# A two-layer diffusion backbone on one core: order of work in layer 1's in-projection and at the program's end

## The chip, the cores and the metric

The kernel runs on one core of a Trainium2 chip. A core has a matrix unit, TensorE (PE in the profile, its weight loads PEld), three engines for elementwise work, VectorE (DVE), ScalarE (ACT) and GpSimd (POOL), and SyncE (SP), which issues most transfers here. Each engine runs its own list of instructions in order and waits on semaphores for the others. The metric is the device time of one execution in microseconds; the kernel before took 2872.38 us, the median of three runs (2871.62 to 2872.77).

## The reference, cut to what matters

The reference sends 1024 latent tokens and 256 context tokens, each 1024 wide, through two layers and a final RMSNorm of the latent tokens. The part that the change touches is layer 1's grouped-query attention up to the first scores, and the end of the program.

```python
hl, hc = modulate(xl, ...), modulate(xc, ...)   # rms_norm(x) * (1 + scale) + shift
pl = hl @ w_in                                  # 8 query heads, 2 key heads, 2 value heads of 128
ql = gqa_q(pl[..., :GQA_Q_W], g_q, cos, sin, True)
kl, vl = gqa_kv(pl[..., GQA_Q_W:], g_k, cos, sin, True)
kc, vc = gqa_kv(hc @ w_in[:, GQA_Q_W:], g_k, cos, sin, False)
ol = attention(ql, concat([kc, kl]), concat([vc, vl])) @ w_out
...
xl = xl + ml[:, 5] * conv_ffn(...)              # a = h @ w_up; (silu(conv(g)) * u) @ w_down
return rms_norm(xl, g_final)
```

Queries and keys are normalised per head over 128 values and then rotated (`apply_rope`); scores of a block are `q k / sqrt(128)`, and their softmax starts with a maximum over the 1280 keys.

## The kernel before, in words

All tokens lie with the model's width on the partitions, in eight tiles of 128 (index k). The tokens form three chunks: two latent ones of 512 columns (c = 0 and 1) and the context of 256 (c = 2). Every product of float32 numbers is made of three matmuls (L72): a value is split into a rounded high part and the rest, and high by high, high by low and low by high are added. So each operand costs a cast for its high part and a subtraction for its low part, besides the matmuls.

The stretches at issue are ordered by hand: inside a region opened with `manual_schedule` each engine executes its work in the order in which the program's calls are written (in the first of the two regions SyncE's transfers are placed by the scheduler, in the second by hand too). So moving a call moves its instructions on every engine that it uses.

*Layer 1's in-projection* is the region that opens at L2276. `Norm` (L1474) makes the RMSNorm and the modulation of one chunk: n0 for chunk 0, n2 for the context, n1 for chunk 1. Its `add` squares a tile on ScalarE (L1489 for the first, L1492 for the others) and adds it to the sum on the engine it is given (L1493); `split` casts the sum (L1505) and makes its low half (L1506); `total` adds over the partitions with a matmul by ones (L203, L204); `root` makes 1/sqrt on ScalarE in three steps, a scaled copy, a logarithm and an exponential (L167, L169, L170), and `rest` a Newton step of three operations on VectorE (L173 to L175). `modulate1` (L225), called in three parts a, b and c_, makes a modulated tile: the scaled value on VectorE (L236), its high part on ScalarE (L243) and its low part on VectorE (L249); for odd tiles of chunk 1 the scaling is on GpSimd (L238, L239) and the low part at L251.

Weights arrive as raw float32 (`wload`, L92); `split(eng)` casts a block's high part on ScalarE (L115) and makes its low part on the engine named (L111). `product(mt, c, ks)` is one block of 128 columns of queries (0 to 7) or keys (8, 9) times a chunk, over the k given, three matmuls each. `Key` and `Query` work on a product: its squares (L2425 for queries) and their split (L2426, L2427; L195, L196 for keys), `stat` with the matmul that sums them (L2436 for queries; L203, L204 for keys), `rope` with three operations on VectorE (L2355, L2358) and a sum on GpSimd (L2362), and `rest`, the Newton step. `value(t, k)` is the value product of token tile t, whose bank is called v, for the last two tiles T; `keep_value` casts it out of the bank (L2465) and makes its low half (L2466). Then attention begins: scores on TensorE (L1197 to L1199), maxima on VectorE (L1220), exponentials on ScalarE (L1237).

Small tiles come from `tmp` by tag: y has two buffers, z one, and some tags have one more from another pool here. A new tile of a tag waits until the last reader of the buffer's former content is done.

*The end* is the region that opens at L2905. It finishes the second layer's ConvFFN and the final norm in three pieces of columns, p (512), q and t (256 each). `prod(d)` is the last part of the down product of tile d (6 matmuls for p, 12 for q or t), `upd` adds it to the stream (L2096, VectorE), `sq` squares it (L2926), `add` sums the squares (L2929), `hi` and `lo` split the sum (L2933, L2936), `total`, `root` and `rest` are as above, `out(d, eng)` scales the tile (L2957 or L2959) and issues its store (L2960), and `pre` is a scaling on ScalarE that `out` on GpSimd needs (L2949).

ScalarE keeps one set of function tables at a time; a function that isn't in it makes an ACT_TABLE_LOAD. `tables(name, pinned)` (L283) asks for a set ahead of its use:

```python
i = S.preload_act_table_set(name)
if pinned:
    tc.keep_in_program_order(i)
```

The set `natural_log_exp_and_others` holds the functions of `root`.

## Time and profile before

| | |
|---|---|
| median of three runs | 2872.38 us (2871.62 to 2872.77) |
| the profiled execution's own time | 2870.99 us |
| its span in the profile | 2869.2 us |
| TensorE busy | 97% of the span |
| VectorE busy | 79% |
| ScalarE busy | 43% |
| GpSimd busy | 24% |
| mean granted clock of TensorE | 0.988 |

The in-projection's stretch of interest runs from 1594.4 to 1767.5 us in the profile, where attention's first exponential starts; the end's region begins on ScalarE at 2814.8 and the span ends at 2869.2. In a view of the timeline a row gives the start, the length, the engine, the line, the operation, the tiles and their shapes, how many instructions of that kind follow each other (xN), and in brackets how long the engine had stood idle and what ended that. In a table of windows each row gives a stretch, its length, and then for TensorE, its weight loads, VectorE, ScalarE and GpSimd the busy time and the number of instructions, then the granted clock (1.00 is the full one) and the share of the transfer engines.

### The profile page before, as it was taken

The numbers are of one execution on the slowest core, as the hardware profiler recorded it, in microseconds if no ns is written. First come the engines' busy times: TensorE is split into PE (matmuls) and PEld (weight loads), VectorE is DVE, ScalarE is ACT, GpSimd is POOL, SyncE is SP. The second block draws the span as 40 slices with busy tenths as digits, with TensorE's granted clock in tenths as the row PEclk, the third lists the DMA queues.
The fourth block names the chain that finished last, engine by engine and source line by source line (L and its number), as shares of the span: only waits on it lengthen the run. The fifth ranks groups of instructions, "written<-read, shape, count | busy, mean of one in ns | idle before, by whom it ended". The sixth has DMA issues, their size and how long they took to land.

```text
span 2869.2 us, 40136 instructions
## 1 busy us (share of the span) xinstructions
PE 2775.6 (97%) x14654; PEld 2318.1 (81%) x14654; DVE 2272.8 (79%) x3886; ACT 1241.0 (43%) x2518; POOL 700.2 (24%) x828
## 2 busy tenths in 40 slices
PE   7988999999999999999999998999999999999997
PEld 3856888887888888888888877999877788888886
DVE  5688888868888888778777787888758777779766
ACT  5525888824433333331002444888734333333104
POOL 2241444763000001011013443444330000001112
PEclk9999999999999999999999999999999999999998
DMA  6144001183143334363221010000041222226211
GB/s 230 71 142 140 15 24 59 57 290 124 41 138 132 126 124 136 132 239 96 69 72 51 29 37 23 1 2 1 27 141 54 81 88 81 75 101 232 92 59 59
DMA packets 97230, 264.89 MB, mean 92 GB/s; under 512 B 11908, under 2 KB 21060, under 8 KB 96904
## 3 DMA queue, kind: packets, MB, share of 16 engines
q1 hardware_dynamic: 97032, 262.33, 27.2%
q8 instruction: 115, 1.88, 0.3%
q14 instruction: 83, 0.68, 0.1%
HBM read 212.53 MB, written 49.75 MB: 91 GB/s over the span
## 4 chain that ended last, share of the span: by engine, by line
PE 64%; DVE 7%; ACT 2%; issue 1%; POOL 1%; DMA 0%; DVEq 0%; SPq 0%; ACTq 0%; POOLq 0%
PE d L72 18%; PE y L72 11%; PE z L72 7%; PE x L72 7%; PE p L72 6%; PE pv L1277 3%; PE b L72 3%; PE T L1264 2%; PE qk L72 1%; PE S L1197 1%; PE S L1199 1%; PE S L1198 1%; PE v L72 1%; DVE x L2014 0%; DVE mx L1220 0%
## 5 line engine op out<-in xcount | busy, mean ns | idle before, releaser
L2096 DVE SCALAR_TENSOR_TENSOR x<-d,mod,x 128x512 f32<-128x512 f32 (+1 forms) x352 | 254.5, 735 | 94.7 <-PE d L72 92.6
L1267 DVE TENSOR_TENSOR tl<-T,th 128x512 fp32r<-128x512 f32 x328 | 225.5, 687 | 46.8 <-ACT th L1266 42.1
L1277 PE MATMUL pv<-th,v 128*128 128x256 f32 x976 | 254.1, 309 | 1.4 <-ACT vo L1406 1.0
L1220 DVE TENSOR_REDUCE mx<-S 128x1 f32<-128x512 f32 (+1 forms) x400 | 233.9, 585 | 10.9 <-PE S L1199 3.7
L1246 POOL TENSOR_SCALAR p<-p,sm 128x1280 f32<-128x1280 f32 x128 | 171.2, 1338 | 288.1 <-DVE sm L1245 190.3
L72 PE MATMUL d<-act,wh 128*128 128x512 f32 (+1 forms) x832 | 231.8, 365 | 0.0
L1266 ACT CAST th<-T 128x512 fp32r<-128x512 f32 x328 | 192.2, 586 | 84.2 <-PE T L1264 76.5
L2079 ACT CAST act<-act 128x512 fp32r<-128x512 f32 (+1 forms) x110 | 61.5, 577 | 382.8 <-PE d L72 222.0
L72 PE MATMUL b<-h,wh 128*128 128x512 f32 (+1 forms) x752 | 206.5, 362 | 6.0 <-DVE h L489 4.1
L1678 POOL TENSOR_SCALAR a1h<-raw 128x1024 fp32r<-128x1024 f32 x38 | 43.2, 1138 | 675.4 <-DMA raw<-in_wup 457.7
L1698 ACT CAST s2h<-x 128x512 fp32r<-128x512 f32 x40 | 24.9, 622 | 392.5 <-PE x L72 254.9
L1264 PE MATMUL T<-ident,p 128*128 128x128 f32 x1280 | 193.0, 272 | 1.6 <-POOL p L1246 1.6
L72 PE MATMUL x<-h,a1h 128*128 128x512 f32 x608 | 191.2, 396 | 0.0
L1264 PEld LDWEIGHTS T<-ident,p 128*128 128x128 f32 x1280 | 156.5, 140 | 34.9 <-POOL p L1246 3.3
L1277 PE MATMUL pv<-tl,v 128*128 128x256 f32 x656 | 177.4, 282 | 0.0
L1277 PEld LDWEIGHTS pv<-th,v 128*128 128x128 f32 x976 | 173.4, 189 | 2.4 <-ACT vo L1406 1.5
L72 PEld LDWEIGHTS d<-act,wh 128*128 128x128 f32 x832 | 149.6, 189 | 27.2
L72 PEld LDWEIGHTS b<-h,wh 128*128 128x128 f32 x752 | 133.0, 189 | 35.8 <-DVE h L489 5.4
L72 PE MATMUL d<-act,wl 128*128 128x512 f32 (+1 forms) x416 | 151.8, 365 | 0.0
L1237 ACT ACTIVATE p<-S,mx,rq 128x512 f32<-128x512 f32 (+1 forms) x192 | 136.2, 712 | 12.7 <-DVE mx L1228 11.2
L72 PE MATMUL b<-h,wl 128*128 128x512 f32 (+1 forms) x376 | 135.8, 361 | 2.4 <-DVE wl L111 2.4
L72 PEld LDWEIGHTS x<-h,a1h 128*128 128x128 f32 x608 | 114.8, 189 | 26.6
(519 smaller groups left out, 7959.1 us busy)
## 6 DMA issues: line engine op xcount, KB each, us to landing
raw<-in_wup SPq DMA_DIRECT2D x86, 512.0 KB, 3.3
wm<-in_wmod SPq DMA_DIRECT2D x72, 512.0 KB, 3.6
act<-d_act SPq DMA_DIRECT2D x88, 256.0 KB, 3.5
raw<-in_wdn SPq DMA_DIRECT2D x44, 512.0 KB, 4.3
raw<-in_wout SPq DMA_DIRECT2D x32, 512.0 KB, 3.5
d_act<-su SPq DMA_DIRECT2D x22, 640.0 KB, 3.8
d_act<-su SPq DMA_DIRECT2D x22, 512.0 KB, 2.6
raw<-in_win SPq DMA_DIRECT2D x20, 512.0 KB, 3.6
```

The lines of the kernel that those rows point to most:

```text
L72: PE.matmul(out, w, x, start=first and i == 0, stop=last and i == n - 1, skip_group_check=more)
L1197: PE.matmul(o, qh, kh[:, ks], start=True, stop=False)
L1220: V.reduce_max(mx[:, j : j + 1], s, axis=AX.X)
L1237: S.activation(o, s, AF.Exp, scale=self.scale, bias=self.mx[:, 3:4], accum_out=self.sm[:, j : j + 1])
L1246: P.tensor_scalar(out=self.p, in0=self.p, scalar1=sm[:, 3:4], scalar2=1.0, op0=ALU.mult, op1=ALU.mult)
L1264: PE.transpose(tb[:, (2 * j + i) * 128 : (2 * j + i) * 128 + 128], rows[i].p[:, c : c + 128], ident)
L1266: S.copy(hi, tb)
L1267: V.tensor_sub(lo, tb, f32(hi))
L1277: PE.matmul(out[0], st, mv, start=(u + j == 0 and x == 0), stop=(u + j == n - 1 and x == len(ops) - 1))
L1678: P.tensor_scalar(out=hi[:, c], in0=self.raw[f, s][:, c], scalar1=1.0, scalar2=0.0, op0=ALU.mult, op1=ALU.add)
L2079: S.copy(hi, f32(lo))
L2096: V.scalar_tensor_tensor(out=x, in0=b, scalar=mod[self.l, c // 2][:, 40 + d : 41 + d], in1=x, op0=ALU.mult, op1=ALU.add)
```

## The change

Seven things are rearranged; every product and every sum stays.

1. The eight `n1.add` calls, of which the first only squares and the others square and add, have their seven sums on VectorE instead of GpSimd. Three calls stand ahead of n2's root and one behind it (three sums, all ahead of n2's Newton step on VectorE), four behind n2's last modulation; before, they were spread between n2's modulations.
2. Key 8's second half of its product with chunk 1, `product(8, 1, range(4, 8))`, stands ahead of `k8_0.stat`, which sums the squares of key 8 and chunk 0.
3. The rope's temporary is of tag z instead of y for queries from head 2 on.
4. Three weight splits stand earlier; `b4_0` stands ahead of `q1_0.stat`, and the statistics of q4_0 and q5_0 behind the product that followed them.
5. `keep_value(4)` and `keep_value(5)` stand together, ahead of the last query's statistics, rope and Newton steps.
6. The end's preload of the tables is pinned to its place in the region.
7. In the end, two more products of t stand ahead of `q.total`; t's sums of squares are all on VectorE; p's and q's outputs are placed later, four of q's behind t's low half, and q's tile 5 is scaled on VectorE.

```diff
--- before.py
+++ after.py
@@ -2348,10 +2348,10 @@
             qtiles[h, c] = hp.tile([128, 512], F32, name="q", tag="h", bufs=HB)
         return qtiles[h, c]
 
-    def rope1(b, c, gcol, dst, n):
+    def rope1(b, c, gcol, dst, n, tag="y"):
 
         c0 = CH[c][0]
-        t = tmp("y", n)
+        t = tmp(tag, n)
         V.scalar_tensor_tensor(out=t, in0=b, scalar=cols[:, gcol : gcol + 1], in1=rc[:, c0 : c0 + n], op0=ALU.mult, op1=ALU.mult)
         for d0 in (0, 64):
             s0 = 64 - d0
@@ -2438,7 +2438,7 @@
                 self.r, self.newton = roots(*i)
 
         def rope(self):
-            rope1(self.b, self.c, G1Q, q_of(self.h, self.c), 512)
+            rope1(self.b, self.c, G1Q, q_of(self.h, self.c), 512, "y" if self.h < 2 else "z")
 
         def rest(self):
             if self.h % 4 == 3:
@@ -2514,39 +2514,35 @@
     value(1, 5)
     value(0, 7)
     n2.total()
-    n1.add(P)
+    n1.add(V)
+    n1.add(V)
+    n1.add(V)
     n2.root()
+    n1.add(V)
     n2.rest()
     n2.a(0, False, "hi")
     n2.b(0)
     value(1, 7)
     value(2, 7)
-    n1.add(P)
     n2.a(1, False, "hi")
     n2.a(2, False, "lo")
-    n1.add(P)
     n2.a(3, False, "lo")
     n2.b(1)
     n2.c_(0)
     n2.b(3)
     n2.b(2)
     n2.c_(1)
-    n1.add(P)
     n2.c_(2)
-    n1.add(P)
     n2.a(4, False, "hi")
     n2.b(4)
     n2.c_(3)
-    n1.add(P)
     b8_0 = product(8, 0, range(0, 8))
     n2.a(5, False, "hi")
     n2.b(5)
     n2.c_(4)
-    n1.add(P)
     n2.a(6, False, "lo")
     n2.b(6)
     n2.c_(5)
-    n1.add(P)
     n2.a(7, False, "lo")
     n2.b(7)
     n2.c_(6)
@@ -2557,6 +2553,10 @@
     value(9, 2)
     value(8, 1)
     n2.c_(7)
+    n1.add(V)
+    n1.add(V)
+    n1.add(V)
+    n1.add(V)
     value(8, 4)
     value(9, 1)
     value(9, 3)
@@ -2615,9 +2615,9 @@
     k8_0 = Key(0, 0, b8_0)
     product(0, 0, range(4, 8), b0_0)
     b8_1 = product(8, 1, range(0, 4))
+    product(8, 1, range(4, 8), b8_1)
     k8_0.stat()
     k8_0.rope()
-    product(8, 1, range(4, 8), b8_1)
     b9_1 = product(9, 1, range(0, 4))
     k8_2 = Key(0, 2, b8_2)
     k8_2.stat()
@@ -2669,12 +2669,12 @@
     product(3, 1, range(4, 8), b3_1)
     q0_1.rope()
     q1_0 = Query(1, 0, b1_0)
+    split(P)
+    b4_0 = product(4, 0, range(0, 4))
     q1_0.stat()
-    split(P)
     q1_0.rope()
     k9_1.rest()
     k9_1.end()
-    b4_0 = product(4, 0, range(0, 4))
     q1_1 = Query(1, 1, b1_1)
     q1_1.stat()
     q1_1.rope()
@@ -2695,17 +2695,17 @@
     q3_0.stat()
     q3_0.rope()
     product(5, 0, range(4, 8), b5_0)
+    split(P)
     q3_0.rest()
     q3_1.stat()
     q3_1.rope()
     q4_0 = Query(4, 0, b4_0)
     q3_1.rest()
-    split(P)
     b5_1 = product(5, 1, range(0, 2))
     product(5, 1, range(2, 6), b5_1)
-    q4_0.stat()
     q4_0.rope()
     product(5, 1, range(6, 8), b5_1)
+    q4_0.stat()
     b6_0 = product(6, 0, range(0, 4))
     q4_1 = Query(4, 1, b4_1)
     split(P)
@@ -2713,9 +2713,9 @@
     q4_1.stat()
     q4_1.rope()
     q5_0 = Query(5, 0, b5_0)
-    q5_0.stat()
     q5_0.rope()
     b6_1 = product(6, 1, range(0, 2))
+    q5_0.stat()
     q6_0 = Query(6, 0, b6_0)
     product(6, 1, range(2, 6), b6_1)
     product(6, 1, range(6, 8), b6_1)
@@ -2735,8 +2735,8 @@
     q6_1.rope()
     product(7, 1, range(2, 6), b7_1)
     q7_0 = Query(7, 0, b7_0)
+    split(P)
     q7_0.stat()
-    split(P)
     q7_0.rope()
     product(7, 1, range(6, 8), b7_1)
     value(4, 0)
@@ -2759,14 +2759,14 @@
     value(4, 6)
     value(4, 7)
     q7_1 = Query(7, 1, b7_1)
-    q7_0.rest()
-    q7_1.stat()
-    q7_1.rope()
     value(5, 5)
     value(5, 7)
     keep_value(4)
+    keep_value(5)
+    q7_1.stat()
+    q7_1.rope()
+    q7_0.rest()
     q7_1.rest()
-    keep_value(5)
     close_ps()
     close_tp()
     close_n()
@@ -2905,7 +2905,7 @@
 
     regions.append(tc.manual_schedule(engines=ENGINES | {mybir.EngineType.SP}))
     regions[-1].__enter__()
-    tables("natural_log_exp_and_others", False)
+    tables("natural_log_exp_and_others")
 
     class Piece:
 
@@ -3031,59 +3031,59 @@
     q.add(7, V)
     q.hi()
     p.out(3, P)
+    t.prod(0)
     q.lo()
-    t.prod(0)
+    t.prod(1)
     p.out(5, P)
     t.upd(0)
     t.sq(0)
-    t.prod(1)
     t.upd(1)
+    t.sq(1)
+    t.prod(2)
+    t.prod(3)
+    q.total()
+    q.root()
+    t.upd(2)
+    t.sq(2)
     p.out(2, V)
-    p.out(4, V)
-    q.total()
-    t.prod(2)
-    t.upd(2)
-    t.sq(1)
-    q.root()
+    t.add(1, V)
+    t.prod(4)
+    t.upd(3)
     q.rest()
-    t.add(1, P)
-    q.out(2, P)
-    t.sq(2)
+    t.sq(3)
     t.add(2, V)
-    t.prod(3)
-    t.upd(3)
-    q.out(0, V)
     p.out(6, P)
-    t.sq(3)
-    p.out(7, P)
-    t.prod(4)
+    t.prod(5)
     t.upd(4)
     t.sq(4)
+    q.out(2, P)
     t.add(3, V)
-    t.prod(5)
+    t.prod(6)
     t.upd(5)
     t.sq(5)
     t.add(4, V)
-    t.prod(6)
-    q.out(7, P)
-    t.add(5, P)
+    p.out(4, V)
+    p.out(7, P)
+    t.prod(7)
     t.upd(6)
-    q.out(1, P)
-    t.prod(7)
     t.sq(6)
-    q.out(5, P)
-    q.out(3, P)
+    t.add(5, V)
     t.upd(7)
     t.sq(7)
     t.add(6, V)
     t.add(7, V)
     t.hi()
     t.lo()
-    q.out(6, V)
+    q.out(7, P)
+    q.out(0, V)
     t.total()
     t.root()
+    q.out(6, V)
+    q.out(1, P)
     q.out(4, V)
+    q.out(3, P)
     t.pre(1)
+    q.out(5, V)
     t.rest()
     t.out(6, V)
     t.out(0, V)
```

On VectorE, where the context chunk's norm ends and its modulations begin and end (x, y, hi, lo and h are tiles of the norm; L111 is a weight's low part, L2466 a kept value):

```order
 L1493 TENSOR_TENSOR x<-x,y 128x256 x2
 L1506 TENSOR_TENSOR lo<-x,hi 128x256
+L1493 TENSOR_TENSOR x<-x,y 128x512 x3
 L173 TENSOR_TENSOR y<-x 128x256
 L174 SCALAR_TENSOR_TENSOR x<-y,x 128x256
```

```order
 L236 SCALAR_TENSOR_TENSOR lo<-xc_12655,mod_66,x 128x256
 L249 SCALAR_TENSOR_TENSOR h<-lo,mod_66,h 128x256 x2
+L1493 TENSOR_TENSOR x<-x,y 128x512 x4
 L111 TENSOR_TENSOR wl<-raw,wh 128x1024
 L2466 TENSOR_TENSOR v_15619<-v,v_15619 128x256
```

Three sums of chunk 1's squares come between the context's low half and its Newton step, four between its last modulation and the weight part; the seven are gone from GpSimd, where they stood ahead of another weight part.

On VectorE, the last query's rope and Newton steps, ahead of attention's first maximum (L1220); v_16748 and v_16751 are the two kept values, v_16765 and v_16771 in the kernel before:

```order
 L2427 TENSOR_TENSOR lo<-y,hi 128x512
+L2466 TENSOR_TENSOR v_16748<-v,v_16748 128x256
+L2466 TENSOR_TENSOR v_16751<-v,v_16751 128x256
+L2355 SCALAR_TENSOR_TENSOR z<-qk,cols,rc 128x512
+L2358 SCALAR_TENSOR_TENSOR q<-qk,cols,rs 64x512 x2
 L173 TENSOR_TENSOR y<-r 128x512
 L174 SCALAR_TENSOR_TENSOR x<-y,x 128x512
 L175 SCALAR_TENSOR_TENSOR r<-x,r 128x512
-L2355 SCALAR_TENSOR_TENSOR y<-qk,cols,rc 128x512
-L2358 SCALAR_TENSOR_TENSOR q<-qk,cols,rs 64x512 x2
-L2466 TENSOR_TENSOR v_16765<-v,v_16765 128x256
```

Both values and the rope now stand ahead of both Newton steps; before, one value stood behind the rope and the other behind the second Newton step.

On ScalarE at the end, p's root (ss is the sum over the partitions):

```order
 L2926 ACTIVATE sq<-x_24966 128x256
 L167 ACTIVATE x<-ss,epst 128x512
-L169 ACT_TABLE_LOAD
-L169 ACTIVATE y<-x 128x512
-L170 ACT_TABLE_LOAD
+L169 ACTIVATE y<-x 128x512
 L170 ACTIVATE r<-y 128x512
```

The two table loads of this root are gone, as they are in the other two roots; one load stands ahead of the region's first square instead, and at the program's start two of four are gone.

## The prediction

> **What bounds the kernel now.** I read the page's busy shares and its chain of waits first, then the table of busy time by stretch, then the rows of the waits in it.
>
> ```profile
> span 2869.2 us, 40136 instructions
> ...
> PE 2775.6 (97%) x14654; PEld 2318.1 (81%) x14654; DVE 2272.8 (79%) x3886; ACT 1241.0 (43%) x2518; POOL 700.2 (24%) x828
> ...
> PE 64%; DVE 7%; ACT 2%; issue 1%; POOL 1%; DMA 0%; DVEq 0%; SPq 0%; ACTq 0%; POOLq 0%
> ```
>
> TensorE is the bound over the whole, so a change can pay only where TensorE waits or runs at a lower granted clock. The stretches that the change touches:
>
> ```profile
> core 0: us, PE busy (x) PEld busy (x) DVE busy (x) ACT busy (x) POOL busy (x), PEclk, DMA share, GB/s
> ...
> 1594.40:1605.10 10.70, 7.58 (x38) 7.13 (x37) 10.70 (x12) 6.13 (x14) 8.21 (x7) 0.68 0.00 0
> ...
> 1626.40:1635.80 9.40, 7.07 (x17) 4.99 (x17) 7.79 (x12) 4.75 (x9) 1.29 (x1) 0.64 0.00 0
> 1635.80:1709.00 73.20, 72.00 (x309) 57.20 (x307) 58.31 (x75) 34.62 (x59) 28.66 (x15) 1.00 0.12 36
> 1709.00:1723.00 14.00, 9.99 (x40) 7.09 (x40) 13.52 (x15) 4.19 (x6) 10.19 (x5) 1.00 0.16 45
> ...
> 1744.80:1767.50 22.70, 15.16 (x95) 13.88 (x94) 14.66 (x22) 4.43 (x10) 4.48 (x4) 0.85 0.08 23
> ...
> 2838.30:2844.10 5.80, 3.30 (x15) 3.11 (x15) 5.18 (x10) 4.55 (x9) 2.63 (x2) 0.71 0.21 77
> ```
>
> TensorE's idle time is 3.1, 2.3, 1.2, 4.0, 7.5 and 2.5 us. The granted clock costs more: 0.68 of 10.7 us is 3.4 us lost to the half clock, 0.64 of 9.4 another 3.4, 0.85 of 22.7 again 3.4 (about 2.5 of it while TensorE works), 0.71 of 5.8 us 1.7. So every idle spell of two microseconds here is followed by a slow spell. All of it in the in-projection is 18.1 + 9.3 = 27 us: that is its ceiling. What ends the waits:
>
> ```profile
> 1596.16 0.50 PE L72 MATMUL v<-wh,h 128*128 128x256 f32 x2 [0.92 <-DVE h L249]
> ...
> 1598.98 0.80 PE L72 MATMUL v<-wh,h 128*128 128x256 f32 x2 [2.20 <-DVE h L249]
> ...
> 1628.61 0.52 PE L203 MATMUL ss<-hi,ones 128*128 128x512 f32 x1 [1.76 <-ACT hi L195]
> ...
> 1746.23 0.39 PE L72 MATMUL v<-wl,h 128*128 128x256 f32 x1 [1.19 <-POOL wl L111]
> ...
> 1757.01 0.58 PE L72 MATMUL T<-wh,h 128*128 128x256 f32 x1 [6.01 <-DVE v L2466]
> ...
> 2840.82 0.58 PE L203 MATMUL ss<-hi,ones 128*128 128x256 f32 x1 [2.50 <-ACT hi L2933]
> ```
>
> **The squares' sums go from GpSimd to VectorE.**
>
> ```profile
> 1592.76 0.48 DVE L249 SCALAR_TENSOR_TENSOR h<-hi,mod,h 128x256 fp32r<-128x256 f32 x1
> ...
> 1597.44 1.48 DVE L249 SCALAR_TENSOR_TENSOR h<-lo,mod,h 128x256 fp32r<-128x256 f32 x1
> ...
> 1607.17 0.67 DVE L1506 TENSOR_TENSOR lo<-x,hi 128x512 fp32r<-128x512 f32 x1
> ...
> 1592.81 7.25 POOL L1493 TENSOR_TENSOR x<-x,y 128x512 f32<-128x512 f32 x5 [10.26 <-ACT y L1492]
> 1601.54 2.95 POOL L1493 TENSOR_TENSOR x<-x,y 128x512 f32<-128x512 f32 x2 [1.49 <-ACT y L1492]
> 1609.38 0.40 PE L203 MATMUL ss<-hi,ones 128*128 128x512 f32 x1
> ...
> 1607.87 2.39 POOL L111 TENSOR_TENSOR wl<-raw,wh 128x1024 fp32r<-128x1024 f32 x1 [3.37 <-ACT wh L115]
> ...
> 2816.91 0.69 DVE L2929 TENSOR_TENSOR x<-x,sq 128x512 f32<-128x512 f32 x1 [0.76 <-ACT sq L2926]
> ```
>
> While GpSimd adds, a 0.48 us modulation takes 1.48: each operation that reads two tiles of SBUF waits for the add. These modulations (chunk 2) are what TensorE waits for at 1596 and 1598.98. The seven adds leave; on VectorE each costs 0.69. Three stand before chunk 2's newton, the last behind a square that follows the root on ScalarE: about 0.55 + 0.69, so the modulations start 1.3 late. Up to 1598.92, where the second wait ends, four stretched operations give back about 3.5, so that point comes at 1596.7. TensorE waits 1.3 where it waited 3.1, too short for a slow spell: 1.8 + 3.4 = 5.2 us ahead at 1605.
>
> Queued behind the other four adds are the split of a weight, four kept values and the low half of chunk 1's sum (1607.17, ended 1607.84). From 1598.92 that was 8.9 us, of which 3.0 stretch leaves and 4 x 0.74 = 2.9 of adds comes: it ends at 1605.5. TensorE, there at about 1604.3, waits some 1.1. Were GpSimd's weight part (2.39, now free to start earlier) first, the low half would come 2 us later and the wait would be 3. Chunk 1's root, newton and modulations follow 4.1 (2.1) sooner.
>
> **The second half of key 8's product ahead of its sum.**
>
> ```profile
> 1628.36 0.69 DVE L251 TENSOR_TENSOR h<-z,h 128x512 fp32r<-128x512 f32 x1
> ...
> 1635.41 0.80 PE L72 MATMUL qk<-h,wh 128*128 128x512 f32 x2
> ```
>
> Its twelve matmuls, 0.23 us each at full clock (2.7 us), now fill the wait at 1628.61, which was 1.76 and then 0.57 us and brought a slow spell of 3.4. In the profile the sum and then this product were through at 1635.41, where the next product begins. The last modulation ended at 1629.0; now it ends 4.1 (2.1) earlier, at 1624.9 (1626.9), and product and sum, which follow it, at about 1627.5 (1629.5). So TensorE begins the next product 7.9 (5.9) us ahead, and in this are the gains of the first part. I take **6.0**, near the bad case, for both parts together; ends 2.5 (another slow spell) and 8.
>
> **Query's rope in z, weights' parts earlier.** The square on ScalarE waited for GpSimd's rope sum to free y:
>
> ```profile
> L2425 ACT ACTIVATE y<-qk 128x512 f32<-128x512 f32 x16 | 9.5, 594 | 17.6 <-POOL q L2362 12.7 <-PE qk L72 2.4 <-POOL z L2362 1.9
> ```
>
> That wait goes; what is late next is VectorE, busy 13.52 of the 14.00 us from 1709, so of TensorE's 4.0 idle I take **2.0** (ends 0 and 4). Splits moved ahead of a root pass three ScalarE operations of some 0.65; of the 1.19 at 1746 I take **0.6** (0 to 1.2). The products moved past statistics move no more than their own time. Against this, TensorE ahead of VectorE, which is busy 58.31 of the 73.20 us after 1635.8, meets its sums later: I give back **2.5** (0 to 5).
>
> **Values kept before the last query.**
>
> ```profile
> 1748.96 0.68 DVE L173 TENSOR_TENSOR y<-r 128x512 f32<-128x512 f32 x1
> ...
> 1756.54 0.42 DVE L2466 TENSOR_TENSOR v<-v,v 128x256 fp32r<-128x256 f32 x1
> 1756.87 0.68 DVE L1220 TENSOR_REDUCE mx<-S 128x1 f32<-128x512 f32 x1
> ...
> 1765.75 0.28 PE L1197 MATMUL S<-k10h,qh 128*128 128x256 f32 x1
> ...
> 1767.53 0.78 ACT L1237 ACTIVATE p<-S,mx,rq 128x512 f32<-128x512 f32 x1 [0.26 <-DVE mx L1228]
> ```
>
> The bank T waits for the second kept value, which stands last, 1756.54. Ahead of it are two newtons and a rope, 7.6 us from 1748.96. Now both values are kept first, at about 1750, and T's matmuls (1757.01 to 1765.75, 8.7 us, less the 2.5 of the slow spell: 6.2) run under that same rope and newtons. VectorE reaches its first maximum as late as before, 1757, but finds T done and the scores behind it at hand: two values at 0.34 and two maxima at 0.68 bring the first exp to about 1760.5 instead of 1767.5. I take **7.0**; ends 4 (a slow spell in T) and 8.5 (all of wait and clock).
>
> In-projection: 6.0 + 2.0 + 0.6 - 2.5 + 7.0 = 13.1.
>
> **The end.**
>
> ```profile
> 2814.82 0.63 ACT L2926 ACTIVATE x<-x 128x512 f32<-128x512 f32 x1 [35.41 <-DVE x L2096]
> ...
> 2829.04 1.28 ACT L169
> ...
> 2830.98 1.28 ACT L170
> ...
> 2857.16 1.28 ACT L169
> ...
> 2858.46 0.42 ACT y L169
> ...
> 2858.95 1.28 ACT L170
> ...
> 2832.94:2856.00 23.06, 16.46 (x121) 15.76 (x119) 20.04 (x35) 15.30 (x32) 14.40 (x13) 0.89 0.33 119
> ```
>
> Each of the three roots now loads two tables (L169, L170), 1.28 us each; the preload that would have spared them stood at the program's start. It now stands in the end region, behind the last casts, where ScalarE waits 35 us for the first square (2814.82): no cost, but 1.28 at the region's head if that wait were gone. The last root's two are on the chain: 2 x 1.28 = **2.6**. The next operation starts 0.02 us after its load (2858.46). The Trainium skill ("ScalarE: Activation LUTs", What ACT_TABLE_LOAD costs) adds a drain of about 1.38 us to every load; by it the last root would give 5.3 instead of 2.6 and the whole sum 20.7 instead of 18.0. The trace shows no such time.
>
> Ahead of it, p's newton starts 2.6 earlier, and VectorE, busy 20.0 of the 23.1 us up to t's low half, carries that on; q's root gives up its loads too, but two adds of 0.4 come from GpSimd. TensorE gets two more products (24 matmuls, 2.9 us) in front of q's sum: its wait of 2.50 and the slow spell of 1.7 go, 4.2 in all, more than VectorE can use; this then waits for nothing, and TensorE waits for it at t's sum. I take **2.3** (0 to 4.2). Four outputs of q moved behind t's low half (0.4 to 0.5 each) fit under t's sum and root, some 2.4 us; the same 24 stores are issued. Together **4.9** (2.6 to 6.8).
>
> At the program's start two loads go, the displaced one and another that the first activation needed because of it:
>
> ```profile
> 11.25 0.63 ACT L184 ACTIVATE x<-xin 128x512 f32<-128x512 f32 x1 [4.19 <-DMA xin<-in_xl]
> ```
>
> ScalarE waits 4.19 us for a transfer behind them, longer than 2 x 1.28: nothing gained; without that wait it would be up to 2.6.
>
> **Sum.** 13.1 + 4.9 = 18.0 us. The profiled execution took 2870.99 us, its span 2869.2; it becomes 2853.0. That execution is 1.4 under the median of the runs, 2872.38, so the median becomes 2854.4.
>
> **Rivals.** (a) *GpSimd's weight part first.* L111 of 2.39 us takes the SBUF pair before chunk 1's low half; TensorE idles 3 us at the sum and a slow spell follows: 2.5 in place of 6.0, and 3.5 given back instead of 2.5, so 13.5 in all: 2858.9. For it: the row 1607.87 starts right behind 1607.17, a matter of 0.7 us, and its cast stands directly behind the sum's on ScalarE. Against it: the wait need not reach two microseconds in one stretch. The Trainium skill ("SBUF — State Buffer", Who interferes with whom) says that whichever of the two engines starts first holds the shared pair for its whole instruction; the stretched modulations agree (1.48 for 0.48).
>
> (b) *Only the end counts.* If attention's first stages, which run from VectorE's maxima and ScalarE's exps, take back what arrives early, 4.9 remain: 2867.5. Against it: after 1767.5 nothing hangs on earlier work but its start.
>
> (c) *VectorE becomes the bound: slower.* If the stretch at 1593 to 1604 is not GpSimd's adds, the seven adds cost 1.48 each as their neighbours did, 10.4, with 1.3 for the late square 11.7 in front of chunk 1's sum, 1.5 of which was slack (1607.84 to 1609.38). Two slow spells more: 10.2 + 6.8 = 17.0 against the 2.0 + 0.6 + 7.0 + 4.9 = 14.5 that stay: 2.5 slower, 2874.9. It decides from 7.7 us on. Against it: the stretch begins and ends with GpSimd's rows.
>
> (d) *The drain of the skill's page*, 20.7 in all: 2851.7.
>
> **How the numbers follow.** Forecast 0.72 (its own range 2849 to 2860), (a) 0.15, (b) 0.06, (c) 0.04, (d) 0.03. Time: that of the forecast, 2854.4. Slow spells of 3.4 us come or stay away by where a wait falls, so the lower end lies two such spells (6.8 us) below the forecast, about 2848, and the upper end takes in (a) and a part of the way to (b), 2863; left out are (b), (c) and the far ends. A difference under 0.2% (5.7 us) can't be told from none here. Faster by more: forecast, (a), (d), 0.90; within: (b), 0.06; slower: (c), 0.04.
>
> **What would show it.** GpSimd without L1493, the chunk 2 modulations all near 0.48, granted clock 1.00 from 1594 to 1605 or nearly; no wait above 1 us at L203 for key 8; T's first matmul within 1 us of the scores before it and the first exp 12 to 14 us earlier; ACT_TABLE_LOAD six times in all instead of thirteen, and the last root some 2.6 shorter. Wrong would be: a wait of over 3 us at chunk 1's sum, slow spells at other places, or VectorE as the releaser of TensorE at more than half of the time saved.

## The result and the profile after

The changed kernel took 2852.26 us in the median of six runs (2850.58 to 2854.36), the kernel before beside it 2872.07 us (2871.11 to 2873.56): 19.8 us less, a ratio of 0.9936 with a 95% interval from 0.9926 to 0.9946. The prediction was 2854.4 us, 18.0 less than before.

The page of the changed kernel, its span and busy shares:

```profile
span 2850.4 us, 40120 instructions
...
PE 2771.3 (97%) x14654; PEld 2313.5 (81%) x14654; DVE 2271.9 (80%) x3896; ACT 1232.4 (43%) x2510; POOL 684.8 (24%) x818
```

TensorE is busy 4.3 us less in a span that is 18.8 us shorter, so most of the gain is waiting time that went, and some 4 us are work done at a higher clock. VectorE has ten operations more (the seven sums, and two sums and an output of the end) and about as much busy time; the operations that GpSimd's sums had stretched are shorter. ScalarE's 8.6 us less are about the seven table loads that went, 1.28 us each. The table of busy time by stretch, with the columns of the one shown before (time, TensorE, weight loads, VectorE, ScalarE, GpSimd, granted clock, share of transfers):

```profile
1594.40:1605.10 10.70, 9.13 (x70) 8.35 (x69) 10.17 (x20) 7.89 (x16) 1.45 (x1) 1.00 0.12 32
1603.10:1611.50 8.40, 5.53 (x18) 4.12 (x17) 5.99 (x10) 2.68 (x5) 2.44 (x2) 0.80 0.40 125
1619.00:1629.00 10.00, 10.00 (x44) 7.87 (x43) 9.10 (x12) 3.67 (x7) 4.25 (x3) 1.00 0.00 0
...
1702.00:1716.00 14.00, 11.89 (x51) 8.91 (x49) 13.75 (x17) 6.74 (x11) 6.91 (x5) 1.00 0.11 39
1716.00:1720.60 4.60, 4.60 (x13) 3.63 (x14) 4.54 (x6) 0.62 (x1) 2.82 (x2) 0.63 0.37 116
1731.00:1754.00 23.00, 21.22 (x143) 18.77 (x141) 17.97 (x29) 9.79 (x19) 7.42 (x5) 1.00 0.09 26
```

The stretch of the context's modulations, which had a clock of 0.68 and 3.1 us of idle TensorE, is at full clock now, and so is the stretch around key 8's sum (0.64 before, 10.00 of 10.00 us busy now) and the one in front of attention (7.5 idle microseconds and a clock of 0.85 before). Two slow spells are new: a clock of 0.80 from 1603.1, and 0.63 from 1716. Both follow a wait, and the timeline's rows say for what:

```profile
1594.19 0.48 DVE L249 SCALAR_TENSOR_TENSOR h<-lo,mod,h 128x256 fp32r<-128x256 f32 x1 [0.19 <-ACT h L243]
...
1603.65 2.34 POOL L111 TENSOR_TENSOR wl<-raw,wh 128x1024 fp32r<-128x1024 f32 x1 [21.86 <-ACT wh L115]
...
1604.01 2.53 DVE L1506 TENSOR_TENSOR lo<-x,hi 128x512 fp32r<-128x512 f32 x1
...
1606.59 0.51 PE L204 MATMUL ss<-lo,ones 128*128 128x512 f32 x1 [2.87 <-DVE lo L1506]
...
1628.25 0.40 PE L203 MATMUL ss<-hi,ones 128*128 128x512 f32 x1
...
1712.97 2.37 POOL L111 TENSOR_TENSOR wl<-raw,wh 128x1024 fp32r<-128x1024 f32 x1
...
1714.08 1.81 DVE L2427 TENSOR_TENSOR lo<-y,hi 128x512 fp32r<-128x512 f32 x1
...
1715.95 0.50 PE L2436 MATMUL ssq<-lo,sel 128*128 128x512 f32 x1 [1.90 <-DVE lo L2427]
...
1753.90 0.78 ACT L1237 ACTIVATE p<-S,mx,rq 128x512 f32<-128x512 f32 x1 [1.93 <-DVE mx L1228]
...
2801.16 0.63 ACT L2926 ACTIVATE x<-x 128x512 f32<-128x512 f32 x1 [34.11 <-DVE x L2096]
```

The modulations take their 0.48 us. But chunk 1's low half (L1506), 0.67 us before, takes 2.53: GpSimd began a weight's low part 0.36 us ahead of it, and VectorE's operation ends 0.55 us after GpSimd's. TensorE waits 2.87 us for it. At 1714 the same happens to a query's low half, 1.81 us for 0.69, again behind a weight's low part, and TensorE waits 1.90 us. At key 8's sum (1628.25) no wait is left. The first exponential starts at 1753.90, where it was 1767.53, and the end's first square at 2801.16, where it was 2814.82.

The end's last root, Newton step and outputs, the stores' row included:

```profile
2835.22 12.09 SPq L2960 DMA_DIRECT2D out_y<-x  x16
```

```profile
2837.33 0.58 PE L203 MATMUL ss<-hi,ones 128*128 128x256 f32 x1 [3.81 <-ACT hi L2933]
...
2838.92 0.42 ACT L169 ACTIVATE y<-x 128x256 f32<-128x256 f32 x1
2839.43 0.42 ACT L170 ACTIVATE r<-y 128x256 f32<-128x256 f32 x1
...
2840.32 1.59 POOL L2957 TENSOR_TENSOR x<-x,r 128x256 f32<-128x256 f32 x2 [1.60 <-ACT x L2949]
2840.33 0.99 DVE L174 SCALAR_TENSOR_TENSOR x<-y,x 128x256 f32<-128x256 f32 x1
2841.44 0.76 DVE L175 SCALAR_TENSOR_TENSOR r<-x,r 128x256 f32<-128x256 f32 x1
...
2845.23 0.41 DVE L2957 TENSOR_TENSOR x<-x,r 128x256 f32<-128x256 f32 x1
```

The Newton step's second and third operation in the kernel before:

```profile
2861.15 0.42 DVE L174 SCALAR_TENSOR_TENSOR x<-y,x 128x256 f32<-128x256 f32 x1
2861.61 0.43 DVE L175 SCALAR_TENSOR_TENSOR r<-x,r 128x256 f32<-128x256 f32 x1
```

The root runs without loads. But two of q's outputs on GpSimd now lie beside the last Newton step, whose second and third operation take 0.99 and 0.76 us instead of 0.42 and 0.43. After VectorE's last operation, 2845.64, SyncE needs 1.67 us more to issue the last of its stores (1.23 before), and the program ends 4.8 us after it; before, 3.7.

### The profile page after: what moved, and what is told of

Read it like the earlier page. It is cut to its first block, busy times and chain, and to the rows that moved or that the text cites. A ratio compares the mean times of both kernels' runs of the same rounds, so it can differ in the third digit from the quotient of the medians.

```text
span 2850.4 us, 40120 instructions
## 1 busy us (share of the span) xinstructions
PE 2771.3 (97%) x14654; PEld 2313.5 (81%) x14654; DVE 2271.9 (80%) x3896; ACT 1232.4 (43%) x2510; POOL 684.8 (24%) x818
## 4 chain that ended last, share of the span: by engine, by line
PE 65%; DVE 6%; ACT 2%; issue 1%; DMA 0%; POOL 0%; DVEq 0%; SPq 0%; ACTq 0%; POOLq 0%
PE d L72 18%; PE y L72 11%; PE z L72 7%; PE x L72 7%; PE p L72 6%; PE pv L1277 3%; PE b L72 3%; PE qk L72 2%; PE T L1264 2%; PE S L1197 1%; PE S L1199 1%; PE S L1198 1%; PE v L72 0%; DVE mx L1220 0%; DVE x L174 0%
## 5 line engine op out<-in xcount | busy, mean ns | idle before, releaser
L1220 DVE TENSOR_REDUCE mx<-S 128x1 f32<-128x512 f32 (+1 forms) x400 | 233.9, 585 | 11.1 <-PE S L1199 3.8
L72 PEld LDWEIGHTS b<-h,wh 128*128 128x128 f32 x752 | 133.7, 190 | 36.2 <-DVE h L489 5.5
```

What stands on the lines that cost most here:

```text
L72: PE.matmul(out, w, x, start=first and i == 0, stop=last and i == n - 1, skip_group_check=more)
L1220: V.reduce_max(mx[:, j : j + 1], s, axis=AX.X)
```

## The experiments

A whole execution of the kernel before varies by several microseconds (2866.16 to 2874.99 in the 28 runs beside the first four experiments), and much of it lies ahead of the change: in the profiles of this study the in-projection's first square starts anywhere from 1538.9 to 1543.2. So each experiment is read by distances within its own profile: from the region's first square (L1489, at 1539.94 before, 1539.18 after) to three points, and in the end's region from its first square (L2926). Point A is the start of key 9's product with chunk 1 (1635.41 before), B the twelfth matmul from the end of the query products (1738.66), C the first exponential (1767.53). The table has the differences from the kernel before, in microseconds, negative where earlier; for the end the durations themselves.

| kernel | A | B | C | end to t's sum | end in all | median (before beside it) | ratio, 95% interval |
|---|---|---|---|---|---|---|---|
| before | 0 | 0 | 0 | 40.8 | 54.4 | | |
| changed | -5.9 | -5.2 | -12.9 | 36.2 | 49.3 | 2852.26 (2872.07) | 0.9936, 0.9926 to 0.9946 |
| part 1 alone, sums on VectorE | -4.5 | -4.7 | -4.5 | 40.8 | 54.4 | 2867.65 (2870.39) | 0.9991, 0.9982 to 1.0000 |
| part 2 alone, key 8's product | -2.8 | -1.2 | -1.2 | 40.8 | 54.2 | 2870.69 (2870.39) | 0.9998, 0.9990 to 1.0007 |
| part 5 alone, values kept first | -2.7 | -2.9 | -9.7 | 40.8 | 54.2 | 2863.15 (2870.39) | 0.9976, 0.9966 to 0.9986 |
| part 6 alone, tables | -0.1 | -0.1 | -0.1 | 37.2 | 48.3 | 2863.02 (2870.39) | 0.9976, 0.9966 to 0.9985 |
| part 7 alone, the end's order | -0.5 | 0.9 | 1.2 | 39.7 | 54.7 | 2872.01 (2871.40) | 1.0003, 0.9994 to 1.0012 |
| changed without part 7 | -5.9 | -5.2 | -12.8 | 37.2 | 48.3 | 2853.12 (2871.54) | 0.9935, 0.9920 to 0.9949 |
| changed without z (part 3) | -5.6 | -5.4 | -13.0 | 36.2 | 48.5 | 2852.19 (2871.54) | 0.9932, 0.9917 to 0.9947 |
| changed without part 4 | -5.6 | -5.1 | -12.0 | 36.2 | 49.1 | 2857.06 (2871.40) | 0.9950, 0.9936 to 0.9963 |
| changed, chunk 1's split first | -8.4 | -7.7 | -15.3 | 36.2 | 49.1 | 2850.30 (2871.54) | 0.9923, 0.9909 to 0.9938 |
| changed, query 5's statistics later | -5.9 | -7.1 | -14.7 | 36.2 | 48.8 | 2853.77 (2871.54) | 0.9935, 0.9919 to 0.9952 |
| both repairs | -8.4 | -9.5 | -17.2 | 36.2 | 49.1 | 2848.87 (2871.40) | 0.9924, 0.9911 to 0.9936 |
| both repairs, the end's old order | -8.5 | -9.6 | -17.2 | 37.2 | 48.3 | 2848.07 (2871.40) | 0.9922, 0.9908 to 0.9935 |

Some expectations give the end's durations 0.1 us shorter (48.2 and 49.2 for 48.3 and 49.3); the table's come from the trace's own last instruction.

Three kernels show how far the points move where nothing is changed. The two that change only the end are at -0.1 and at -0.5 to 1.2. The kernel with the values kept first changes nothing ahead of A, and has A 2.7 us sooner. The waits are nearly the same in all of them, but a slow spell follows a wait in one execution and not in another. So a difference of up to 2.7 us at A, in one profile of a kernel near the kernel before, need not be the change's. Kernels with the changed kernel's first two parts agree better at A: -5.6 to -5.9 in five profiles, -8.4 to -8.5 in the three that repair chunk 1's sum.

### The sums on VectorE, alone

```diff
     n2.total()
-    n1.add(P)
+    n1.add(V)
+    n1.add(V)
+    n1.add(V)
     n2.root()
+    n1.add(V)
     n2.rest()
...
     n2.c_(7)
+    n1.add(V)
+    n1.add(V)
+    n1.add(V)
+    n1.add(V)
```

> The kernel before with part 1 alone: chunk 1's seven sums of squares on VectorE. In the changed kernel's trace TensorE is 5.4 us ahead after the context's modulations, then waits 2.9 us for chunk 1's low half, which VectorE cannot finish while GpSimd makes a weight part, and runs a slow spell; 0.6 us are left of the 5.4. Theory: that loss is covered, because chunk 1's modulations still come about 2 us sooner and TensorE finds key 8's sum ready instead of waiting 1.8 us with a slow spell behind: 4 to 5 us ahead at key 9's product, 2.5 to 4.5 us at the program's end. Rival 1, the loss stays: 0.6 us, no difference. Rival 2, the gain belongs to part 2 (the product ahead of the sum): about 2 us.

The view of waits of this kernel, TensorE from 1590 to 1640 (microseconds in total, times, longest):

```profile
PE ss L204 <- DVE lo L1506: 2.9, 1, 2.9
PE ss L204 <- DVE lo L196: 0.6, 1, 0.6
PE ss L203 <- ACT hi L195: 0.5, 1, 0.5
```

The same 2.9 us behind GpSimd's weight part are there, TensorE loses them and a slow spell, and still A comes 4.5 us sooner: the wait at key 8's sum (L203) falls from 1.76 to 0.5 with no slow spell behind it, since VectorE's modulations come sooner. What a wait costs depends on whether the engine waited for is the late one at the next meeting too; here VectorE was, and the loss was covered. The theory fits this profile, and the 0.6 us of rival 1 do not. How much of the 4.5 us is the slow spell at key 8's sum, which can stay away without the change, one profile cannot say; the medians are 2.7 us apart, with an interval from 0 to 5.2.

### Key 8's product ahead of the sum, alone

```diff
+    product(8, 1, range(4, 8), b8_1)
     k8_0.stat()
     k8_0.rope()
-    product(8, 1, range(4, 8), b8_1)
```

> The kernel before with part 2 alone: the second half of key 8's product ahead of the sum. Theory: twelve matmuls (2.8 us) fill waits of 1.8 and 0.6 us and the slow spell (1.7 us lost) goes: 4 us ahead at key 9's product, 2.4 to 4 us at the end. With part 1 alone that makes more than the 5.9 us that both together show there, so the two share their gain. Rival, the parts add up: 5.9 less what part 1 gives alone.

A came 2.8 us sooner, less than the 4 expected; this execution was 0.95 us behind at the context's modulations already, for which the part can't be blamed. The waits at the sum are gone, and TensorE waits 1.44 us for VectorE's last modulations inside the product instead. But 2.8 us is about what A also moves with nothing changed. So A does not decide whether the two parts share their gain (4.5 and 2.8 alone, 5.9 together) or add up, as the rival has it. Some 15 us later TensorE meets VectorE again, at the sum of key 9 and the context; here in the kernel before and in the changed one:

```profile
1650.67 0.39 PE L204 MATMUL ss<-lo,ones 128*128 128x256 f32 x1 [0.18 <-DVE lo L196]
```

```profile
1645.57 0.39 PE L204 MATMUL ss<-lo,ones 128*128 128x256 f32 x1 [0.56 <-DVE lo L196]
```

Counted from the region's first square, the changed kernel is 4.3 us ahead here, part 1 alone 4.7 and part 2 alone 1.2. Behind this place the product ahead of the sum adds nothing to the sums on VectorE: what TensorE is further ahead at A it waits for here. The times see no difference between part 2 alone and the kernel before.

### Values kept first, alone

```diff
-    q7_0.rest()
-    q7_1.stat()
-    q7_1.rope()
     value(5, 5)
     value(5, 7)
     keep_value(4)
+    keep_value(5)
+    q7_1.stat()
+    q7_1.rope()
+    q7_0.rest()
     q7_1.rest()
-    keep_value(5)
```

> The kernel before with part 5 alone: both values kept ahead of the last query's statistics, rope and Newton steps (with the rope's temporary in z for head 7, which this order needs). Theory: T's matmuls begin about 6 us sooner, no slow spell, the first exponential 7 to 8 us sooner, and the same at the end. Rival, the gain needs TensorE and VectorE as far ahead as the other parts bring them: about 4 us.

The cut leaves out the rope's temporary in z for head 7. From B to C this kernel is 6.9 us shorter, the changed one 7.6; the rival with 4 falls. C itself is 9.7 sooner, because 2.7 were won ahead of A, where nothing of this part stands. Its row of the sum at key 8, the window around it, and its first exponential:

```profile
1622.00:1631.00 9.00, 6.67 (x28) 4.88 (x27) 7.92 (x10) 5.38 (x9) 3.19 (x4) 1.00 0.00 0
```

```profile
1627.53 0.50 PE L203 MATMUL ss<-hi,ones 128*128 128x512 f32 x1 [1.74 <-ACT hi L195]
...
1756.81 0.78 ACT L1237 ACTIVATE p<-S,mx,rq 128x512 f32<-128x512 f32 x1 [1.92 <-DVE mx L1228]
```

The wait is the same, 1.74 us here and 1.76 in the profile before, but there the clock fell to 0.64 behind it and here it stays at 1.00. So a wait of this length brings a slow spell in some executions and not in others, and a price for it is right only on the average.

### The tables alone, and the end's order alone

```diff
-    tables("natural_log_exp_and_others", False)
+    tables("natural_log_exp_and_others")
```

> The kernel before with part 6 alone: the preload of the tables pinned in the end's region. Theory: the last root is 2.6 us shorter, and p's and q's roots earlier by as much bring VectorE ahead by about 1 us: 3 to 4 us from the end region's first square to the end of the span. Rival 1: the earlier roots bring nothing, 2.6 us. Rival 2: all of the end's 5.2 us come from the tables and none from the new order.

The last root of the kernel before (first and last operation, the loads lie between) and of this kernel:

```profile
2856.67 0.47 ACT L167 ACTIVATE x<-ss,epst 128x256 f32<-128x256 f32 x1 [1.13 <-PE ss L204]
...
2860.24 0.42 ACT L170 ACTIVATE r<-y 128x256 f32<-128x256 f32 x1
```

```profile
2855.44 0.47 ACT L167 ACTIVATE x<-ss,epst 128x256 f32<-128x256 f32 x1 [1.13 <-PE ss L204]
2855.95 0.42 ACT L169 ACTIVATE y<-x 128x256 f32<-128x256 f32 x1
2856.46 0.42 ACT L170 ACTIVATE r<-y 128x256 f32<-128x256 f32 x1
```

It takes 1.44 us to the end of its third operation; before, 3.99 (2856.67 to 2860.66), so 2.55 or twice 1.28 went. But the end as a whole got 6.1 us shorter, more than any of the three answers expected: 3.6 up to t's sum (2.6 of them at q's sum already) and 2.6 behind it. p's root with its two loads was on the path as well, since VectorE waits for it with q's sums, and a part of q's loads too. The second rival was nearest, and low: the tables alone give more than the changed kernel's end gained.

The end's order with the loads left in place:

> The kernel before with part 7 alone: the end's new order, the tables not pinned, so that every root loads its tables. Theory: t's sum comes about 1 us sooner, and the last Newton step and the stores take that back: the end takes 53.5 to 54.5 us (54.4 before). Rival: the new order is worth the 2.3 us that the prediction gave to the end ahead of t's sum: 52 us.

t's sum came 1.1 us sooner; from there to the start of the third operation of the last Newton step it took 0.65 us more, that operation and the stores behind it took the rest, and the end took 54.7 us against 54.4. The theory's direction holds, and the time lies 0.2 above its bounds.

### The changed kernel with the end's old order

```diff
     tables("natural_log_exp_and_others")
...
-    t.prod(0)
     q.lo()
-    t.prod(1)
+    t.prod(0)
     p.out(5, P)
...
```

> The changed kernel without part 7: the end in its old order, the tables pinned. With the tables alone the end took 48.2 us from its first square to the end of the span, in the changed kernel 49.2. Theory: the new order takes 1.0 us more than it gives, since q's outputs behind t's low half stretch the last Newton step (0.65 us) and queue ahead of t's stores on SyncE; this kernel's end takes 48.2 and the rest is as in the changed kernel. Rival: the order pays once the in-projection comes earlier too: 49.2 or more.

48.3 us, as with the tables alone. The changed kernel's order took 48.5 to 49.3 in the six profiles that have it; t's sum is 1.0 us sooner there in each, VectorE's last operation no sooner (44.5 us from the region's first square in both orders), and behind that the old order needs 3.7 us and the new one 4.1 to 4.8. SyncE's issuing of the last stores explains 0.2 to 0.5 of that (1.4 to 1.7 us against 1.2); the rest was not followed. In whole executions that is too little to be seen.

### Without z, and without part 4

```diff
-            rope1(self.b, self.c, G1Q, q_of(self.h, self.c), 512, "y" if self.h < 2 else "z")
+            rope1(self.b, self.c, G1Q, q_of(self.h, self.c), 512, "z" if self.h == 7 else "y")
```

> The changed kernel with part 3 undone except for head 7 (where the new order of the end of the in-projection needs it): the rope's temporary in y. Theory: the squares wait for GpSimd's sums again; query 6's product, 9.4 us ahead of the kernel before in the changed one, is 4 to 6 us ahead, and the first exponential 1 to 2 us later than in the changed kernel. Rival: all that z brings is given back by VectorE before the first exponential: within 0.5 us of the changed kernel there.

The rival holds in these profiles: 13.0 us at C without z and 12.9 with it. On the way the part does what it says (in the stretch before query 6's product the kernel with z is 1.4 us ahead), but VectorE is busy 13.75 of 14.00 us there, and TensorE only comes sooner to query 5's statistics. There it waits 1.90 us with a slow spell behind; without z it waits 0.53 us and then 1.09, with none:

```profile
1717.55 0.50 PE L2436 MATMUL ssq<-lo,sel 128*128 128x512 f32 x1 [1.09 <-DVE lo L2427]
```

For part 4 its lines of the change were undone, those of the splits, `b4_0` and the statistics of queries 4 and 5:

> The changed kernel without part 4: the weights' splits, a product and two statistics where they were. Theory: the part is worth little: the first exponential 0 to 1 us later than in the changed kernel. Rival: it made the wait at query 5's statistics (1.9 us and a slow spell); without it the first exponential comes 1 to 2 us sooner.

0.85 us at C, inside the theory's bounds. The rival falls, since the wait at query 5's statistics is there without part 4 too:

```profile
1718.66 0.50 PE L2436 MATMUL ssq<-lo,sel 128*128 128x512 f32 x1 [2.15 <-DVE lo L2427]
```

Without part 4 TensorE also waits 1.4 and 1.1 us for weights' low parts on GpSimd, where the changed kernel waits 0.4 at the second place alone. The 0.85 may be too low a price, though. Behind these 2.15 us the clock stayed at 1.00, while the changed kernel lost 1.7 us to a slow spell behind its 1.90 (a clock of 0.63 over 4.60 us); with equal luck the part would be worth up to some 2.5 us, an estimate from these rows. The median is 4.8 us above the changed kernel's. In the profile 2.4 us more lie ahead of the region and 1.3 between attention and the end, where both kernels run the same work; a slow spell right behind the first exponential (a clock of 0.57 from 1758 to 1766) belongs to the latter, and the rest is open.

### Two repairs

```diff
+    n1.split()
     keep_value(0)
     keep_value(1)
     keep_value(2)
     keep_value(3)
     value(9, 7)
-    n1.split()
```

> The changed kernel with chunk 1's split written ahead of the first four kept values, so that VectorE makes the low half (0.69 us) before GpSimd begins its weight part. Theory: the wait of 2.9 us at chunk 1's sum falls under 0.5, the slow spell behind it goes, and chunk 1's root and modulations come 2 us sooner: key 9's product and the first exponential 1.5 to 2.5 us ahead of the changed kernel. Rival 1: TensorE then waits at key 8's modulations instead, which VectorE sets, under 1 us. Rival 2: the values' banks come free later, and TensorE waits for one of them: 0.

```profile
1602.69 0.68 DVE L1506 TENSOR_TENSOR lo<-x,hi 128x512 fp32r<-128x512 f32 x1
...
1603.77 0.50 PE L203 MATMUL ss<-hi,ones 128*128 128x512 f32 x1 [0.39 <-DVE v L2466]
...
1604.42 2.41 POOL L111 TENSOR_TENSOR wl<-raw,wh 128x1024 fp32r<-128x1024 f32 x1 [22.62 <-ACT wh L115]
```

The low half now takes 0.68 us, with nothing beside it on GpSimd, the wait is 0.39, and A and C come 2.5 us sooner than in the changed kernel. So it was the weight part that stretched it. A wait of 1.5 us for VectorE's modulations at key 8's product is what is left, as the first rival said, but without its price.

```diff
-    q5_0.stat()
     q6_0 = Query(6, 0, b6_0)
     product(6, 1, range(2, 6), b6_1)
+    q5_0.stat()
```

> The changed kernel with query 5's statistics on TensorE twelve matmuls (2.8 us) later. In the changed kernel TensorE waits there 1.9 us for a low half that VectorE finishes late behind GpSimd's weight part, and a slow spell follows (1.7 us lost). Theory: both go, 3 us ahead at the last query's product, 1 to 3 us at the first exponential. Rival: VectorE, busy 13.75 of the 14.00 us there, sets the pace, and the wait comes back at the next statistics: under 0.5 us at the first exponential.

The window after the place, and the two waits that took over, from the view of waits:

```profile
1714.00:1724.00 10.00, 9.48 (x42) 7.29 (x41) 9.85 (x12) 2.34 (x4) 7.67 (x4) 1.00 0.16 53
```

```profile
PE ssq L2436 <- DVE lo L2427: 1.0, 3, 0.5
PE qk L72 <- DVE q L2358: 0.8, 1, 0.8
```

The spell is gone and the wait divided; B and C both come 1.8 us sooner than in the changed kernel (3 expected near B). VectorE does set the pace, as the rival said, but not the whole of it. In whole executions it does not show: the median is 2853.77 us, beside 2852.19 and 2853.12 for the kernels without z and without part 7.

This profile also shows what the slow spell at chunk 1's sum costs:

```profile
1609.85 0.50 PE L204 MATMUL ss<-lo,ones 128*128 128x512 f32 x1 [2.88 <-DVE lo L1506]
...
1628.85 0.50 PE L72 MATMUL qk<-h,wh 128*128 128x512 f32 x1 [1.49 <-DVE h L249]
```

The wait at the sum is that of the changed kernel, but the clock behind it stayed at 1.00 (0.80 there), and A is -5.9 in both: TensorE came sooner to key 8's product and waited 1.49 us for VectorE's modulation, where the changed kernel has no wait. So up to A the spell cost nothing; what cost was the late low half on VectorE, which the first repair moves.

### Both repairs, with either end

> The changed kernel with both repairs (chunk 1's split ahead of the first kept values, query 5's statistics twelve matmuls later) and the end in its old order with the tables pinned. Theory: the two repairs act at different places and add up: the first exponential 2.5 + 1.8 = 4.3 us ahead of the changed kernel; the end takes 48.2 us, 0.3 to 1.0 less. Some 5 us faster than the changed kernel, 23 us faster than the kernel before. Rival: VectorE, further behind TensorE, takes back the second repair: 2.5 to 3 us at the first exponential.

> The changed kernel with both repairs and its own end. Theory: as the kernel with the old end up to the first exponential; the end takes 48.5 to 49.2 us, 0.3 to 1.0 more than the old order. Rival: no difference between the two ends.

```profile
1751.27 0.78 ACT L1237 ACTIVATE p<-S,mx,rq 128x512 f32<-128x512 f32 x1 [2.25 <-DVE mx L1228]
...
2797.65 0.63 ACT L2926 ACTIVATE x<-x 128x512 f32<-128x512 f32 x1 [34.11 <-DVE x L2096]
```

These two rows are of the kernel with the old end; its span is 2845.9 us. The repairs add up: 17.2 us at C against 12.9 (4.3 sooner), with either end, and the ends take 48.3 and 49.1 us. The medians, 2848.07 and 2848.87 us, are 4 and 3 us under the changed kernel's; each was measured beside its own runs of the kernel before (23.3 and 22.5 us under them), so between the two ends the times decide nothing and the profiles show 0.8 us. Both have lower medians than both kernels of the comparison; the runs with the old end (2847.12 to 2850.24) all lie under those of the changed kernel (2850.58 to 2854.36).

## Why the prediction was right, point by point

| term of the sum | predicted | measured |
|---|---|---|
| squares' sums and key 8's product, up to A | 6.0 | 5.9 |
| z, less what is given back, A to B | 2.0 - 2.5 = -0.5 | -0.7 |
| weights' parts and values kept before the last query, B to C | 0.6 + 7.0 = 7.6 | 7.6 |
| in-projection | 13.1 | 12.9 |
| the end | 4.9 | 5.1 |
| sum | 18.0 | 18.0 |

The spans differ by 18.8 us; the remaining 0.8 is the start of the in-projection's region, which varies by more than that from execution to execution, and the medians' 19.8 lies a little above.

**The squares' sums and key 8's product: right at A, by the forecast's bad case.** The stretched modulations went as said (0.48 us each, 5.4 ahead after them where 5.2 was predicted). Then rival (a)'s mechanism came: GpSimd's weight part began first, and the wait at chunk 1's sum was 2.87 us with a slow spell, where the forecast had 1.1 and its bad case 3. The bad case made 5.9 us at A, and 5.9 was measured. The price of (a) did not come: it took 3.5 us off this term for the slow spell, but a profile without that spell has the same A, because VectorE's modulations set it. The repair shows what the collision did cost: 2.5 us, as the low half came late. The term's second half is weaker than its number: 1.6 of the 5.9 us are gone at key 9's sum, and from there the product ahead of key 8's sum adds nothing to the sums on VectorE.

**z and what is given back: the net by luck.** The net from A to B is -0.7 us where -0.5 was predicted, but it is made of other sizes. TensorE gives back 1.6 us up to key 9's sum, wins 5.1 up to query 6's product, where it is 9.4 ahead, and loses 4.2 behind that by the wait of 1.90 us at query 5's statistics, another weight part's work, and its slow spell. z was put at 2.0 and is worth 0 at C. The step that failed is the one that let half of TensorE's idle time at 1709 be won while VectorE was busy 13.5 of 14.0 us. The rule read from the first profile, that every idle spell of two microseconds is followed by a slow spell, failed too: waits of 2.88 and 2.15 us were not.

**The weights' parts: right where they were read.** The wait of 1.19 us at 1746, of which 0.6 was taken, is 0.4 in the changed kernel, and without part 4 the stretch from B to C is 0.7 us longer.

**The values: right.** T's first matmul waits 0.3 us, its matmuls run beside the rope and the Newton steps, and B to C is 7.6 us shorter, 6.9 with this part alone.

**The end: right sum by luck, wrong split.** The last root's 2.6 us were right (2.55). The other 2.3 were put down to p's newton and, for the larger part, to the products in front of q's sum. The runs show the tables at 6.1 us in all, 1.2 more than the whole term, and the new order at -0.3 alone and -1.0 behind the tables; the two misses cancel. The step that failed is that q's four outputs "fit under t's sum and root": two of them on GpSimd stretch the Newton step by 0.9 us, and the program ends 0.4 to 1.1 us later behind VectorE's last operation.

**The rivals.** (b) fell, since the 12.9 us at C were kept to the end's first square (13.66 less the 0.76 of the region's start). (c) fell: the seven sums took 0.69 us each on VectorE. (d), a drain behind every table load as the Trainium skill has it ("ScalarE: Activation LUTs", What ACT_TABLE_LOAD costs), would have made the last root some 5.3 us shorter, an estimate from that page's figures; taking away its two loads took away 2.55, the loads' own time, so no drain shows in these traces. The program's start gave nothing that can be told from the start's own spread.

The signs named in the prediction came as listed: no sums on GpSimd, no wait above 1 us at key 8's sum, the first exponential 13.6 us earlier, six table loads. Of the signs against it one came, two slow spells at new places; the repairs at these places gave 2.5 and 1.8 us.

## What to carry to other kernels

Price a wait at the next place where the two engines meet: if the engine waited for is late there too, the wait is already paid, and two cures for the same lateness share their gain. So compare two kernels behind that place, and not at the point that a change was made for: 1.6 of 5.9 us were gone some 15 us later. When work leaves a shared resource, look for what starts earlier because of it: here the weight's part that followed the sums on GpSimd moved into the way of the very operation that the move was to free, and writing one call five lines higher gave 2.5 us. Measure a reordering apart from a cure that it is bundled with: the pinned tables carried the whole gain of the end, and the order took some of it back.

## What the runs showed of the hardware

TensorE waits of about the same length at the same place were followed by a slow spell in one profile and not in another. At key 8's sum it was 1.76 us with a granted clock of 0.64 behind it, and 1.74 us with 1.00. At chunk 1's sum it was 2.87 us with 0.80, and 2.88 us with 1.00. At query 5's statistics it was 1.90 us with 0.63, and 2.15 us with 1.00. What decides was not tried.

VectorE's operations that read two tiles of SBUF and came up while GpSimd ran ended the same time after GpSimd's operation in each case read here: 0.55 us for 512 columns (L1506, 2.53 us instead of 0.67, and L2427, 1.81 instead of 0.69), 0.28 us for 256 (L174 in the last Newton step, 0.99 instead of 0.42). So a small operation can pay most of the other engine's length.
